# Accumulators of one PSUM bank, sums of squares added as they come, and three smaller edits in an encoder block

## The chip, the cores and the metric

The kernel runs on one core of a Trainium2 chip. Its time is the device time of one execution, in microseconds (us), and the median of several runs is what counts. Engines are called PE (TensorE, matmuls), ACT (ScalarE), DVE (VectorE), POOL (GpSimd) and SP (SyncE, which issues the DMAs).

## What is computed

One layer of an encoder on 256 positions with 2048 features, in float32. In short:

```
def reference(x, ...):
    hn = rmsnorm(h, mix_norm_pre)
    z, xbc, dt_raw, u = split(hn @ w_in)              # 1024, 1536, 32, 1024 columns
    y_ssd  = ssd_mixer(z, xbc, dt_raw, ...)            # scan in both directions, 16 heads
    y_pool = pool_mixer(u, pool_w, pool_scale)         # centred means of 4 widths, minus u
    h = h + rmsnorm(concat(y_ssd, y_pool) @ w_out, mix_norm_post)
    hn = rmsnorm(h, ffn_norm_pre)
    gate, val = split(hn @ w_ffn_up)                   # 5632 columns each
    ff = (gelu(dwconv(gate)) * val) @ w_ffn_down
    h = h + rmsnorm(ff, ffn_norm_post)
    g = sigmoid(rmsnorm(h, ple_norm_pre) @ w_ple_gate)
    return h + rmsnorm(g * (p @ w_ple), ple_norm_post)
```

`rmsnorm` divides each position by the root of the mean of its squares. All weights come from HBM in float32.

## The kernel before

Every product is made of three: a float32 matrix is split into a high part (cast on ACT, tiles `...whi`) and the rest (subtracted on DVE, `...wlo`), and PE multiplies high by high, high by low and low by high. Activations are split in the same way by `put` (ACT writes `...h`, DVE `...l`). Raw weights come by DMA from SP into four buffers (`raw`); the parts go to five buffers each.

The stages in order of time: the first product `dtu` (the columns `dt` and `u` of `w_in`), `xbc` in three slabs (2, 0, 1), `z`, the output projection `wo` (accumulator `woa`), the FFN's up projection (`ug` and `uv`, accumulators `ga` and `va`), the down projection `dn` (accumulators `dna`, `dns`), and the gate (`gt`). `ple` is a small product that does not depend on the rest and lies between these stages.

Matmuls write to PSUM, which has eight banks of 512 float32 a partition. `main` and `pair_of_banks` give tiles of two banks, of which there are three; `misc` gives one of two tiles of one bank. The program is written in order; dependences and the order on each engine are made by the framework, which tracks who reads and writes a tile as a whole: a reader of one half of a tile can be held by a writer of the other half. Beside the long products, small jobs (the list `work`, one entry a unit of the product) are called by `aside`: `pool_mix` makes the pooled means (`mx`), `pool_map` their product (`pw`), `seg(i)` one pair of exponent matrices, which share the two `misc` tiles with them.

`sublayer` makes `wo` and `dn`. It works on two halves of the 2048 columns, and in each on two blocks `t` of 128 positions and two banks `n`. For each bank ACT squares the accumulator and sums it (`woj`, sum in `woq`) and DVE multiplies it by the gain (`wom`). After both halves `rms` adds four sums for each block on POOL (L366, tiles `wo0m`, `wo1m`) and raises the result to the power −1/2 (L369, `wo0r`, `wo1r`). Then DVE adds the scaled result to `h` (L820), PE transposes `h` (`woxt`, for `dn` `dnxt`), and `put` makes the panel (`wox`, `dnx`) for the next product. `row_rstd` sums the squares of the new `h` on ACT (`rfj`), and `along_tokens` turns the factor into a row (`rfbw`, `rfbp`).

`feature_pairs` makes 256 columns of the up projection for all positions: its accumulator holds high and low products of 256 positions each beside one another in each bank, and `total` adds them: ACT copies one part out of PSUM, DVE adds the other.

## Time and profile before

| | |
|---|---|
| Time, median of 3 runs | 1131.77 us (1130.02, 1131.77, 1133.52) |
| Profiled execution | 1130.95 us, its span 1129.2 us |
| Busy: PE, DVE, ACT, POOL | 1112.7, 798.6, 662.1, 52.0 us |
| Chain that ended last: PE, DVE, ACT, DMA | 92%, 3%, 3%, 1% |

In the rows of the profile the first number of a timeline row is its start in us from the start of the span, the second its duration; then come engine, line, operation, names of output and inputs, shapes, and in brackets how long the engine had been idle before and which engine and tile it waited for. A row with "x8" stands for eight instructions. Windows give start and end, the length, then busy time and instruction count of PE, PE's weight loads, DVE, ACT and POOL, then the clock, the DMA share and GB/s. Rows of waits give total time, how often, and the longest. Rows of grouped instructions (by line and shape) give the total busy time in us, the mean of one in ns, and idle time before them. Rows of loads give the KB of each and the median us from issue to landing.

### The profile page before, as it was taken

To read this page: it belongs to the slowest core of one execution; us is meant where nothing else is said; L and a number is where in the kernel's file an instruction comes from. 1 tells how busy PE (TensorE), PEld (TensorE's weight loads), DVE (VectorE), ACT (ScalarE), POOL (GpSimd) and SP (SyncE) were. 2 spreads that over 40 slices of the span, in tenths; PEclk is the share of its full clock that TensorE was granted. 3 is DMA by queue.
4 is the path that set the end of the run, shared out by engine and by line. 5 is a ranking of instruction groups with operands and counts; after the bars stand their busy time and mean duration, and the time that the engine had idled before them with its cause. 6 is when DMAs were issued, how large, how long until landed. Compare 5 with 4: busy or idle time off the path is not lost.

```text
span 1129.2 us, 15491 instructions
## 1 busy us (share of the span) xinstructions
PE 1112.7 (99%) x6031; PEld 968.1 (86%) x6031; DVE 798.6 (71%) x937; ACT 662.1 (59%) x933; POOL 52.0 (5%) x80
## 2 busy tenths in 40 slices
PE   9999999999899999999999999999999999999996
PEld 9999988888788888888888888888888888887885
DVE  6658877754767777767767676666777778787573
ACT  6747774543675565655656555646656466567462
POOL 0300023100100000000000000000000000001001
PEclk9999999999999999999999999999999999999998
DMA  9944356666577878887797697666788788885742
GB/s 354 385 153 150 114 184 203 234 185 198 187 259 253 270 263 254 264 296 250 254 318 246 224 319 259 196 196 201 258 291 284 251 276 322 302 286 192 238 135 75
DMA packets 143993, 270.43 MB, mean 239 GB/s; under 512 B 5296, under 2 KB 98352, under 8 KB 140592
## 3 DMA queue, kind: packets, MB, share of 16 engines
q1 hardware_dynamic: 143632, 269.09, 71.0%
q8 instruction: 47, 0.77, 0.3%
q10 hardware_dynamic: 288, 0.36, 0.1%
q14 instruction: 26, 0.21, 0.1%
HBM read 247.93 MB, written 21.50 MB: 239 GB/s over the span
## 4 chain that ended last, share of the span: by engine, by line
PE 92%; DVE 3%; ACT 3%; DMA 1%; issue 1%; POOL 1%; POOLq 0%; DVEq 0%; ACTq 0%
PE va L91 22%; PE ga L91 21%; PE dna L91 15%; PE woa L91 7%; PE gt L91 7%; PE xbc L91 6%; PE dns L91 5%; PE z L91 4%; PE dtu L91 2%; DMA dtur<-w_in 1%; PE pw L91 1%; PE yd L91 1%; DVE h_back L820 0%; PE seg L91 0%; ACT rxj L395 0%
## 5 line engine op out<-in xcount | busy, mean ns | idle before, releaser
L91 PE MATMUL ga<-wox,ug_0whi 128*128 128x512 f32 x352 | 88.6, 394 | 1.5 <-DVE wox L201 1.5
L91 PE MATMUL va<-wox,uv_0whi 128*128 128x512 f32 x352 | 87.6, 391 | 0.0
L91 PE MATMUL ga<-wox,ug_1whi 128*128 128x512 f32 x352 | 87.5, 390 | 0.0
L91 PE MATMUL va<-wox,uv_1whi 128*128 128x512 f32 x352 | 87.0, 390 | 0.0
L91 PEld LDWEIGHTS va<-wox,uv_1whi 128*128 128x128 f32 x352 | 66.1, 188 | 13.7
L91 PEld LDWEIGHTS ga<-wox,ug_1whi 128*128 128x128 f32 x352 | 66.0, 188 | 13.6
L91 PEld LDWEIGHTS ga<-wox,ug_0whi 128*128 128x128 f32 x352 | 64.9, 190 | 14.0 <-DVE wox L201 1.7
L91 PEld LDWEIGHTS va<-wox,uv_0whi 128*128 128x128 f32 x352 | 64.7, 188 | 12.5
L91 PE MATMUL ga<-wox,ug_1wlo 128*128 128x256 f32 x352 | 50.2, 284 | 0.0
L91 PE MATMUL ga<-wox,ug_0wlo 128*128 128x256 f32 x352 | 49.5, 283 | 0.0
L91 PE MATMUL va<-wox,uv_1wlo 128*128 128x256 f32 x352 | 49.4, 284 | 0.0
L91 PE MATMUL va<-wox,uv_0wlo 128*128 128x256 f32 x352 | 49.3, 283 | 0.0
L91 PEld LDWEIGHTS ga<-wox,ug_0wlo 128*128 128x128 f32 x352 | 46.8, 191 | 1.7
L91 PEld LDWEIGHTS va<-wox,uv_0wlo 128*128 128x128 f32 x352 | 46.7, 191 | 1.7
L91 PEld LDWEIGHTS ga<-wox,ug_1wlo 128*128 128x128 f32 x352 | 45.6, 192 | 0.3 <-ACT wox L200 0.3
L91 PEld LDWEIGHTS va<-wox,uv_1wlo 128*128 128x128 f32 x352 | 45.4, 192 | 0.0
L91 PE MATMUL xbc<-hnh,xb_0whi 128*128 128x256 f32 x96 | 28.1, 293 | 0.2 <-DVE u L539 0.2
L91 PE MATMUL xbc<-hnh,xb_1whi 128*128 128x256 f32 x96 | 27.5, 286 | 0.0
L366 POOL TENSOR_SCALAR dn0m<-dnq,fmean 128x1 f32<-128x1 f32 x1 | 0.3, 264 | 589.9 <-ACT dnj L810 589.9
L91 PE MATMUL xbc<-hnh,xb_0wlo 128*128 128x256 f32 x96 | 27.3, 285 | 0.0
L91 PE MATMUL xbc<-hnl,xb_1whi 128*128 128x256 f32 x96 | 27.2, 283 | 0.0
L91 PE MATMUL xbc<-hnh,xb_1wlo 128*128 128x256 f32 x96 | 27.2, 283 | 0.0
(1427 smaller groups left out, 3016.0 us busy)
## 6 DMA issues: line engine op xcount, KB each, us to landing
dn0r<-w_ffn_down SPq DMA_DIRECT2D x16, 1024.0 KB, 6.8
dn1r<-w_ffn_down SPq DMA_DIRECT2D x15, 1024.0 KB, 6.4
br<-w_ffn_down SPq DMA_DIRECT2D x13, 1024.0 KB, 5.6
bm<-block SPq DMA_DIRECT2D x13, 1024.0 KB, 6.3
zr<-w_in SPq DMA_DIRECT2D x8, 1024.0 KB, 5.3
wo0r<-w_out SPq DMA_DIRECT2D x8, 1024.0 KB, 6.0
wo1r<-w_out SPq DMA_DIRECT2D x8, 1024.0 KB, 5.6
gt0r<-w_ple_gate SPq DMA_DIRECT2D x8, 1024.0 KB, 5.9
```

Of the source, the lines that this page charges most:

```text
L91: nc.tensor.matmul(o, lhsT, rhs, start=start, stop=stop, skip_group_check=True)
L366: nc.gpsimd.tensor_scalar(m, q, scale, base, op0=ALU.mult, op1=ALU.add)
```

## The change

Accumulators from `main` become two tiles of one bank each, of which the pool has six, where there were three of two banks. `pair_of_banks` goes; `feature_pairs` writes to `acc[f]`, and `total` works on each bank by itself. `sublayer` adds each sum of squares on POOL as it comes and takes the power behind the last sum of each block. One `seg` stands in each unit of `xbc`, and `pool_map` is spread with it. The second part of `x` (`xt1`) lies in one of the four raw weight buffers. `pool_mix` has its matmuls put behind the last matmul ahead of it in the program.

```
--- before.py
+++ after.py
-            tc.tile_pool(name="pmain", bufs=3, space=bass.MemoryType.PSUM) as pm, \
+            tc.tile_pool(name="pmain", bufs=6, space=bass.MemoryType.PSUM) as pm, \
...
         def main(name):
-            t = pm.tile([P, 1024], F32, tag="main", name=name)
-            return [t[:, :512], t[:, 512:]]
-
-        def pair_of_banks(name):
-            return pm.tile([P, 1024], F32, tag="main", name=name)
+            return [pm.tile([P, 512], F32, tag="main", name=f"{name}_{i}") for i in range(2)]
...
         def mm(o, lhsT, rhs, start, stop):
-            nc.tensor.matmul(o, lhsT, rhs, start=start, stop=stop, skip_group_check=True)
+            last["pe"] = ins(nc.tensor.matmul(o, lhsT, rhs, start=start, stop=stop, skip_group_check=True))
...
-        xt = [ep.tile([P, V_SCW + L], F32, name="xt0")] + [page(f"xt{i}") for i in (1, 2)]
+        xt = [ep.tile([P, V_SCW + L], F32, name="xt0")] + [wp.tile([P, 2048], F32, tag="raw", bufs=4, name="xt1"), page("xt2")]
...
         def total(o, acc):
 
-            v, w = o.rearrange("p (f t) -> p f t", f=2), acc.rearrange("p (f q t) -> p q f t", f=2, q=2)
-            nc.scalar.copy(v, w[:, 1])
-            nc.vector.tensor_add(v, v, w[:, 0])
+            for f in range(2):
+                nc.scalar.copy(o[:, f * L:(f + 1) * L], acc[f][:, L:])
+                nc.vector.tensor_add(o[:, f * L:(f + 1) * L], o[:, f * L:(f + 1) * L], acc[f][:, :L])
...
         def pool_mix(g):
             ps = misc(f"mx{g}")
+            behind = last["pe"]
             for c in range(2):
                 for s, (t0, t1) in enumerate(((0, P + 8), (P - 8, L))):
-                    mm(ps[:, c * L + t0:c * L + t1],
-                       ut[:, s * 1024 + g * 256 + c * P:s * 1024 + g * 256 + (c + 1) * P],
-                       pmat[:, (2 * g + s) * L + t0:(2 * g + s) * L + t1], s == 0, s == 1)
+                    with tc.issue_after(behind):
+                        mm(ps[:, c * L + t0:c * L + t1],
+                           ut[:, s * 1024 + g * 256 + c * P:s * 1024 + g * 256 + (c + 1) * P],
+                           pmat[:, (2 * g + s) * L + t0:(2 * g + s) * L + t1], s == 0, s == 1)
...
         work.extend([
-            [job(seg, 0), job(seg, 1), job(pool_map, 0), job(pool_map, 1)],
+            [job(seg, 0), job(pool_map, 0)],
+            [job(seg, 1), job(pool_map, 1)],
             [job(seg, 2), job(cb, bc, 0), job(cb, bc, 1)],
-            [job(seg, 3), job(seg, 4), job(pool_map, 2)],
-            [job(seg, 5), job(pool_map, 3)],
+            [job(seg, 3), job(pool_map, 2)],
         ])
         xa = xbc(0)
         work.extend([
-            [job(seg, 6), job(scale_by_dt, 0, 0, 0)],
-            [job(seg, 7), job(scale_by_dt, 0, 0, 1), job(weigh, 0, 0)],
-            [job(xs_turn, xa, 0)],
-            [],
+            [job(seg, 4), job(pool_map, 3), job(scale_by_dt, 0, 0, 0)],
+            [job(seg, 5), job(scale_by_dt, 0, 0, 1), job(weigh, 0, 0)],
+            [job(seg, 6), job(xs_turn, xa, 0)],
+            [job(seg, 7)],
         ])
...
             mg = [page(f"{name}m{t}") for t in range(2)]
-            sq = [[], []]
+            mean, r = list(base), []
             for half in range(2):
...
                         nc.scalar.activation(junk, b, AF.Square, accum_out=q)
                         nc.vector.tensor_mul(mg[t][:, c], b, gain[:, c])
-                        sq[t].append(q)
+                        m = tiny(f"{name}m{t}{half}{n}", 1)
+                        nc.gpsimd.tensor_scalar(m, q, 1.0 / D, mean[t], op0=ALU.mult, op1=ALU.add)
+                        mean[t] = m
+                    if half:
+                        r.append(tiny(f"{name}r{t}", 1))
+                        nc.gpsimd.tensor_tensor(r[t], mean[t], mhalf[:, :1], op=ALU.pow)
             if ahead:
                 ahead()
-            r = [rms(f"{name}{t}", sq[t], 1.0 / D, 1, base[t]) for t in range(2)]
             pan = panel(f"{name}x")
```

In `feature_pairs`, `acc[:, f * 512:(f + 1) * 512]` becomes `acc[f]`, and `ga` and `va` come from `main`. Lines move by up to four.

On PE, the place between `dtu` and the first slab of `xbc`: `rxbp` turns the factors of the first norm, `mx` is the pooling. Before:

```order
L91 MATMUL rxbp<-ident,rxbw_607 128x128
L91 MATMUL rxbp<-ident,rxbw_610 128x128
L91 MATMUL mx_764<-pmat,u 128x136
L91 MATMUL xbc_647<-hnh_115,xb_0whi 128x256
L91 MATMUL xbc_647<-hnl_117,xb_0whi 128x256
```

After:

```order
L87 MATMUL rxbp<-ident,rxbw_610 128x128
L87 MATMUL rxbp<-ident,rxbw_613 128x128
L87 MATMUL xbc_0_650<-hnh_118,xb_0whi 128x256
L87 MATMUL xbc_0_650<-hnl_120,xb_0whi 128x256
L87 MATMUL xbc_0_650<-hnh_118,xb_0wlo 128x256
```

The `mx` matmul no longer stands ahead of the first `xbc` matmul; all of them come behind the unit.

On PE, the end of the output projection. `woxt` are transposes of `h` (before `h_2068` is block 0 and `h_2069` block 1, after `h_2076` and `h_2077`). Before, the 22 `ple` matmuls from the end of `woa` to the first transposes, of which the last rows are shown:

```order
L91 MATMUL ple_2798<-ple_0whi,pth 128x512
L91 MATMUL ple_2798<-ple_0wlo,pth 128x512
L91 MATMUL ple_2798<-ple_0whi,ptl 128x512
L91 MATMUL ple_2798<-ple_1whi,pth 128x512
L380 MATMUL woxt_2718<-ident,h_2068 128x128
L380 MATMUL woxt_2727<-ident,h_2068 128x128
L91 MATMUL ple_2798<-ple_1wlo,pth 128x512
L91 MATMUL ple_2798<-ple_1whi,ptl 128x512
L380 MATMUL woxt_2718<-ident,h_2069 128x128
L380 MATMUL woxt_2718<-ident,h_2068 128x128
L380 MATMUL woxt_2718<-ident,h_2069 128x128
L380 MATMUL woxt_2727<-ident,h_2069 128x128
```

After, from the last `woa` matmul on:

```order
L87 MATMUL woa_1_2423<-wo_1whi,catl_2071 128x512
L376 MATMUL woxt_2730<-ident,h_2076 128x128
L376 MATMUL woxt_2739<-ident,h_2076 128x128
L87 MATMUL ple_0_2809<-ple_0whi,pth 128x512
L87 MATMUL ple_0_2809<-ple_0wlo,pth 128x512
L87 MATMUL ple_0_2809<-ple_0whi,ptl 128x512
```

And, still on PE, after these and seven more `ple` matmuls:

```order
L87 MATMUL ple_1_2810<-ple_1wlo,pth 128x512
L87 MATMUL ple_1_2810<-ple_1whi,ptl 128x512
L376 MATMUL woxt_2730<-ident,h_2077 128x128
L376 MATMUL woxt_2730<-ident,h_2076 128x128
L376 MATMUL woxt_2730<-ident,h_2077 128x128
L376 MATMUL woxt_2739<-ident,h_2077 128x128
```

Two transposes of block 0 now stand right behind `woa`, and 12 `ple` matmuls lie between them and the transposes of block 1.

On DVE, the same place. `wom` is the accumulator times the gain (before `wom_2074` is block 0 and `wom_2075` block 1, after `wom_2082` and `wom_2083`), `ug_..wlo` are splits of the FFN's first weights. Before:

```order
L811 TENSOR_TENSOR wom_2074<-woa_2402,gmix 128x512 x2
L157 TENSOR_TENSOR ug_1wlo<-ug00r_2902,ug_1whi 128x1024
L811 TENSOR_TENSOR wom_2075<-woa_2403,gmix 128x512
L157 TENSOR_TENSOR ug_0wlo<-ug00r_2944,ug_0whi 128x1024
L811 TENSOR_TENSOR wom_2075<-woa_2403,gmix 128x512
L820 SCALAR_TENSOR_TENSOR h_2068<-wom_2074,wo0r,h_2068 128x512
L820 SCALAR_TENSOR_TENSOR h_2069<-wom_2075,wo1r,h_2069 128x512
L820 SCALAR_TENSOR_TENSOR h_2068<-wom_2074,wo0r,h_2068 128x512
```

After:

```order
L809 TENSOR_TENSOR wom_2082<-woa_0_2420,gmix 128x512
L809 TENSOR_TENSOR wom_2082<-woa_1_2421,gmix 128x512
L822 SCALAR_TENSOR_TENSOR h_2076<-wom_2082,wor_2708,h_2076 128x512 x2
L809 TENSOR_TENSOR wom_2083<-woa_0_2422,gmix 128x512
L822 SCALAR_TENSOR_TENSOR h_2076<-wom_2082,wor_2708,h_2076 128x512
L809 TENSOR_TENSOR wom_2083<-woa_1_2423,gmix 128x512
L822 SCALAR_TENSOR_TENSOR h_2077<-wom_2083,wor_2722,h_2077 128x512 x3
L197 SCALAR_TENSOR_TENSOR wox_2724<-woxt_2730,vt,wox_2724 128x256
```

The first two updates of `h` of block 0 stand ahead of block 1's `wom`, and the two splits between the `wom` rows have moved behind all of `h` and the first four `wox`.

More of the change, by code (lines that the diff above doesn't have):

```diff
@@ L336, in high @@
                     for k, f, s in block(u, j):
-                        mm(acc[:, f * 512:(f + 1) * 512], wh[:, s], get.both(k), k == 0, False)
+                        mm(acc[f], wh[:, s], get.both(k), k == 0, False)
             def low(u, tiles):
@@ L341, in low @@
                     for k, f, s in block(u, j):
[L342 removed]
+                        mm(acc[f][:, L:], wl[:, s], get(k)[0], False, False)
             def block(u, j):
@@ L910, in build @@
             for i in range(2):
-                ga = pair_of_banks(f"ga{s}{i}")
+                ga = main(f"ga{s}{i}")
                 feature_pairs(f"ug{s}{i}", w_up, s * 512 + i * 256, hf, ga)
@@ L924, in build @@
             for i in range(2):
-                va = pair_of_banks(f"va{s}{i}")
+                va = main(f"va{s}{i}")
                 feature_pairs(f"uv{s}{i}", w_up, DFF + s * 512 + i * 256, hf, va)
```

1 line of the change is left out of this document (removed).

## The prediction

> **What bounds the kernel now.** I read the page first, then busy time by stage, then PE's waits, then the timeline at the places where it waits.
>
> ```profile
> PE 1112.7 (99%) x6031; PEld 968.1 (86%) x6031; DVE 798.6 (71%) x937; ACT 662.1 (59%) x933; POOL 52.0 (5%) x80
> 46.00:145.00 99.00, 97.78 (x739) 94.27 (x739) 71.34 (x119) 66.50 (x115) 0.40 (x2) 1.00 0.50 169
> 290.00:330.00 40.00, 36.15 (x196) 29.89 (x195) 30.57 (x46) 28.21 (x46) 5.33 (x11) 0.96 0.69 230
> 330.00:794.00 464.00, 464.00 (x2678) 411.30 (x2677) 328.37 (x363) 268.15 (x360) 0.00 (x0) 1.00 0.78 255
> 1017.00:1040.00 23.00, 22.12 (x110) 17.42 (x109) 19.84 (x31) 15.41 (x31) 3.65 (x8) 1.00 0.57 179
> PE ga L91 <- DVE wox L201: 1.5, 1, 1.5
> PE woxt L380 <- DVE wox L201: 1.5, 3, 0.8
> PE rfbp L91 <- DVE rfbw L406: 0.5, 1, 0.5
> PE mx L91 <- ACT u L538: 0.3, 1, 0.3
> PE xbc L91 <- DVE u L539: 0.2, 1, 0.2
> ```
>
> The first row is busy time over the span of 1129.2 us: PE works 99% of it, so work that lies beside PE is free and a gain has to come out of PE's idle time. The windows show where that is. In the FFN, 330 to 794 us, PE is busy 464.00 of 464 us. It is idle for 3.85 us between 290 and 330 (from the output projection to the FFN), 1.22 between 46 and 145, 0.88 between 1017 and 1040, and for the rest at the two ends. The waits name them: the transposes and first products behind `wox`, one row each for `rfbp`, `mx` and `xbc`. The change leaves the number of matmuls alone, so its whole effect has to appear in these few us, or as new idle time.
>
> The profiled execution took 1130.95 us against 1131.77, the median of the runs. I make the sum in its times and take the difference from the median.
>
> **The start of xbc.** `pool_mix` no longer puts the first `mx` matmul in front of `xbc`, and `xbc`'s first bank needs one reader gone, not all four of a two-bank tile.
>
> ```profile
> 52.54 0.61 PE L91 MATMUL rxbp<-ident,rxbw 128*128 128x128 f32 x4
> 52.90 0.53 ACT L538 ACTIVATE u<-dtu,rx0r 128x320 f32<-128x320 f32 x1 [1.98 <-DVE dt L537]
> 53.46 0.58 DVE L539 TENSOR_SCALAR u<-dtu,rx0r 128x352 f32<-128x352 f32 x1 [0.52 <-ACT u L538]
> 53.48 0.50 PE L91 MATMUL mx<-pmat,u 128*128 128x136 f32 x2 [0.33 <-ACT u L538]
> 54.19 0.36 PE L91 MATMUL xbc<-hnh,xb_0whi 128*128 128x256 f32 x1 [0.21 <-DVE u L539]
> ```
>
> PE ends `rxbp` near 53.0, waits for ACT's `u` (52.90) to do `mx`, then for DVE's `u` (53.46) to free the tile of `xbc`, which starts at 54.19. In the new order `xbc` stands right behind `rxbp`, and its bank is that of `dtu2` for token block 0 (the first 128 tokens), whose `u` is now ACT's first: the matmuls of that block stand 1.4 us ahead of `rxbp` in PE's order, so the bank is free. Start 53.0 in place of 54.19, less 0.23 for the two `mx` matmuls that PE does later: 0.96 us. The exponent pairs are spread one to a unit, and `pw0` takes the place of the second pair behind the same ACT copy, so I leave the other stalls of this stage (1.22 idle in all, counting the 0.54 above) as they are. Bounds: −0.2, if they grow by what the start wins, to −1.8, if all idle time but small change goes.
>
> **From the projection to the FFN.** Accumulators of one bank let the first sum of squares start when its own bank is done; the mean is built as sums come, the power follows the last sum of its block, and in DVE's new order `h` stands ahead of the splits of `ug`.
>
> ```profile
> 284.08 0.39 PE L91 MATMUL woa<-wo_1whi,catl 128*128 128x512 f32 x1
> 285.93 0.60 ACT L810 ACTIVATE woj<-woa 128x512 f32<-128x512 f32 x1 [1.73 <-PE woa L91]
> 287.38 0.60 ACT L810 ACTIVATE woj<-woa 128x512 f32<-128x512 f32 x1 [0.76 <-DVE wom L811]
> 288.23 0.26 POOL L366 TENSOR_SCALAR wo0m<-woq,wo0m 128x1 f32<-128x1 f32 x1 [1.17 <-ACT woj L810]
> 288.58 0.57 POOL L369 TENSOR_TENSOR wo0r<-wo0m,mhalf 128x1 f32<-128x1 f32 x1
> 288.16 0.39 PE L91 MATMUL woa<-wo_1whi,catl 128*128 128x512 f32 x1
> 289.05 1.23 DVE L157 TENSOR_TENSOR ug_1wlo<-ug00r,ug_1whi 128x1024 fp32r<-128x1024 f32 x1 [0.26 <-ACT ug_1whi L156]
> 289.23 1.09 POOL L366 TENSOR_SCALAR wo1m<-woq 128x1 f32<-128x1 f32 x1
> 292.52 0.74 DVE L820 SCALAR_TENSOR_TENSOR h<-wom,wo0r,h 128x512 f32<-128x512 f32 x1
> 292.58 1.10 POOL L369 TENSOR_TENSOR wo1r<-wo1m,mhalf 128x1 f32<-128x1 f32 x1
> 293.72 0.75 DVE L820 SCALAR_TENSOR_TENSOR h<-wom,wo1r,h 128x512 f32<-128x512 f32 x1 [0.45 <-POOL wo1r L369]
> 296.91 1.15 PE L91 MATMUL ga<-wox,ug_0whi 128*128 128x512 f32 x2 [1.51 <-DVE wox L201]
> 310.41 1.97 ACT L395 ACTIVATE rfj<-h 128x2048 f32<-128x2048 f32 x1
> 313.79 0.46 PE L91 MATMUL rfbp<-ident,rfbw 128*128 128x128 f32 x2 [0.52 <-DVE rfbw L406]
> ```
>
> Today bank 0's last matmul starts at 284.08, yet its `woj` waits until 285.93, when bank 1 is done; bank 1's `woj` waits for DVE's `wom` of bank 0, to 287.38. So `wo0r`, the factor of token block 0, comes at 289.15, the first columns of `h` of block 0 at 293.26 (behind two splits and `wom`), those of block 1 at 294.47.
>
> Step by step after: `woj` of bank 0 at 284.5, of bank 1 at 285.9, 1.45 before today's 287.38, and the factor with it: 287.7. `h` of block 0, now next on DVE, is written by 288.5 (0.74 each), when PE leaves `woa` (288.55): its two transposes hardly wait. Block 1: its last `woj` stands behind one cast on ACT and ends near 289.75; the mean step and the power, between the rows with and without a neighbour on DVE (0.26 to 1.09 and 0.57 to 1.10), give its factor between 290.7 and 292.1. I take 291.2, one of the two at the long row, and `h` of block 1 at 292.0. PE fills until 291.5 with 12 `ple` matmuls and waits 0.5. The 6 transposes, 11 `ple`, 8 more transposes and 8 `ga` then run to about 298.1 without a gap (today `ga` starts at 296.91 with 8 transposes fewer done). What is late next: the splits of `ug`, moved behind, now stand before the `wox` for which the transposes `woxt8` wait, 1.2 us more. ACT reaches `rfj`, the row sums of `h`, some 2.1 us sooner than 310.41, since its `wox` and `pl` come sooner. So `rfbp` starts at 311.7 and not at 313.79, and in the new order five matmuls of 512 columns and one of 256 more stand ahead of it (5 × 0.227 + 0.12 = 1.25 us by the distance of their starts): 2.1 + 1.25 = 3.3 us. Bounds: −1.5, if the next wait on DVE takes all but the transposes that need no wait, to −4.2, a bit over the idle time of this window with the refill after each wait.
>
> **From the down projection to the gate.** The same change of `sublayer`.
>
> ```profile
> 1020.31 0.60 ACT L810 ACTIVATE dnj<-dna 128x512 f32<-128x512 f32 x1 [0.93 <-DVE dnm L811]
> 1025.67 0.74 DVE L820 SCALAR_TENSOR_TENSOR h_back<-dnm,dn0r,h_back 128x512 f32<-128x512 f32 x1
> 1026.00:1030.00 4.00, 3.48 (x18) 2.30 (x17) 4.00 (x8) 3.42 (x6) 0.00 (x0) 1.00 0.99 357
> 1035.37 0.73 PE L91 MATMUL gt<-gt_1wlo,dnxh 128*128 128x512 f32 x2 [0.36 <-DVE gt_1wlo L157]
> ```
>
> `h_back` could start at about 1024.1 in place of 1025.67, but DVE is full (4.00 of 4.00 us), so an earlier `h_back` only pushes the split of `gt_0` (1.21 us) behind it, and the 17 `ple` matmuls that cover this place stay as many. PE begins its transposes 1.5 us sooner and then waits for `gt_0wlo` and the next `dnxl`, where it waits for a split today (1035.37). I count 0; −1.2 if the idle time here goes, +0.9 if the split costs a wait of its own size less what is won.
>
> **Edits costed at nothing.** `total` makes two copies and two additions of 256 columns out of one each of 512, 44 times.
>
> ```profile
> L359 ACT COPY gr<-ga 128x512 f32<-128x512 f32 x22 | 12.9, 588 | 15.9 <-PE ga L91 15.9
> L200 ACT ACTIVATE wox<-woxt,vt 128x256 fp32r<-128x256 f32 x16 | 7.1, 478 | 4.1 <-PE woxt L380 3.1 <-DVE wox L201 1.0
> L360 DVE TENSOR_TENSOR gr<-gr,ga 128x512 f32<-128x512 f32 x22 | 15.1, 688 | 1.5
> L645 DVE TENSOR_TENSOR cbm<-small,cbm 128x256 f32<-128x256 f32 x4 | 1.5, 422 | 0.5 <-ACT cbm L643 0.5
> ```
>
> ACT: 2 × 0.478 − 0.588 = 0.37 us more each, DVE: 2 × 0.422 − 0.688 = 0.16. That is 16.2 us of ACT and 6.9 us of DVE, on engines with 268 and 328 of 464 us busy; the cover is PE's unbroken 464 us, and without it they cost up to 23 us (below). The Trainium skill ("VectorE: DVE Perf Modes", section on the TRN2 errata) speaks against this edit: a fixed cost is paid by each instruction, so tiles should be of 512 elements or more. Its formula for an fp32 addition, (N+151)/0.96 ns, gives 0.157 us more for each pair, an estimate that agrees with the 0.16 of the rows; the sum by it would still be 0 while PE covers it.
>
> Half of `x` in a weight buffer: the loads of the first product have one buffer less and three are issued up to 2.8 us later.
>
> ```profile
> dtur<-w_in SPq DMA_DIRECT2D x14, 528.0 KB, 10.1
> 29.77 1.08 ACT L156 CAST dtu12whi<-dtur 128x1056 fp32r<-128x1056 f32 x1
> 41.02 0.64 PE L91 MATMUL dtu<-dtu12whi,hnh 128*128 128x352 f32 x3
> ```
>
> A load takes 10.1 us from issue to landing, and the loads land one by one, so most of that is waiting behind others and a later issue moves its landing by less; and `dtu12`, cast at 29.77, is first used at 41.02. The cover is about 8 us; the price without it is what goes beyond. SP issues the first `uv` load behind two stores of `h`, but its first use is a whole pair of `ga` products away. At the end, the `tanh` of block 1's first bank could start sooner, but the last bank's chain, which ends the span, starts with the last matmul as before: 0.
>
> **Sum.** −0.96 − 3.3 + 0 = −4.3 us: 1126.7 for the profiled execution, 1127.5 on the median. 0.3%, about what a measurement here can tell from no change, is 3.4 us.
>
> **Rivals.**
>
> R1, the wait moves: with `h` of block 0 now on DVE while POOL makes block 1's factor, both of POOL's steps take the long rows, the factor comes at 292.1, and all behind it, DVE's queue included, is 0.9 later: 2.4 won in place of 3.3. At the gate it costs 0.9 in the same way. −0.96 − 2.4 + 0.9 = −2.5: 1129.3. For it speak `wo1m` (1.09) and `wo1r` (1.10) beside DVE's work on SBUF; against it that DVE, waiting for the factor, lets POOL through. The Trainium skill ("GPSIMD Engine Reference", "Key points") says that GpSimd contends with VectorE instructions with two SBUF inputs; the rows agree (0.26 beside `wom`, which reads PSUM, 1.09 beside the split), and by that rule R1 is the case.
>
> R2, slower: the FFN's covers fail. If each `total` holds the casts and splits queued behind it, and PE waits for weights by that much, 44 × (0.37 + 0.16) = 23 us: 1150.6. It decides from (3.4 + 4.3) / 44 = 0.175 us a `total` on. Against it: PE shows no wait at all in this window, and ACT and DVE idle over a quarter of it. The rule on small tiles of the Trainium skill ("VectorE: DVE Perf Modes", section on the TRN2 errata) leads to this time, were these engines the bound.
>
> R3, all idle time goes: the gate gives 1.2 and xbc 1.8: −6.3, 1125.5. For it: an earlier `h_back` by 1.5 us; against: DVE full there.
>
> **How the numbers follow.** Forecast 0.54, R1 0.26, R3 0.11, R2 0.09. The forecast's own range is −2.8 to −5.6, of which about 0.09 falls short of 3.4 us. So faster 0.45 + 0.11 = 0.56, same 0.09 + 0.26 = 0.35, slower 0.09. The range adds the bounds of the three places: −1.8 − 4.2 − 1.2 = −7.2 and −0.2 − 1.5 + 0.9 = −0.8, that is 1124.6 to 1131.0, and 0.5 on both sides for the median's own scatter (1130.02 to 1133.52 before): 1124.1 to 1131.5. It leaves out R2 and the ends of the others.
>
> **What would show it.** Right: `xbc` starting at 53.0 with no wait for `mx`; the `woj` of 285.93 at 284.5; `h` from 287.7 on; `rfbp` 2 us sooner; 330 to 794 without PE idle, two 128x256 additions near 0.42 us in it. Wrong: a wait of PE for `wox` as long as today's, `wor1` at or over 1.1 us, PE idle in the FFN, or `dtu` weights that PE waits for before 50 us.

## The result, and the profile after

The changed kernel took 1125.95 us (median of 6 runs, 1125.63 to 1127.74) beside 1131.68 for the kernel before on the same chip: a ratio of 0.9953, with a 95% interval of 0.9940 to 0.9965: about 0.5% faster, which is clear of the scatter. Its profiled execution took 1125.82 us, its span is 1124.0 us.

Where the 5.2 us of span come from is read best as distances between the same PE instructions in the two traces (start to start, from the timeline of PE). The last column is the first experiment below, the one-bank accumulators alone.

| From … to (first or last matmul of the name) | before | after | change | banks alone |
|---|---|---|---|---|
| start … first `rxbp` | 52.54 | 52.50 | −0.04 | 52.60 |
| first `rxbp` … last `z` | 144.09 | 143.60 | −0.49 | 142.83 |
| last `z` … last `woa` | 91.53 | 91.53 | 0 | 91.53 |
| last `woa` … first `va` | 38.83 | 35.32 | −3.51 | 34.33 |
| first `va` … last `va` | 466.53 | 466.53 | 0 | 466.53 |
| last `va` … last `gtz` | 326.45 | 325.39 | −1.06 | 325.27 |
| last `gtz` … end | 9.18 | 9.12 | −0.06 | 9.12 |

The row of busy times from the page, the window of the FFN and some of PE's waits in the changed kernel:

```profile
PE 1109.0 (99%) x6031; PEld 965.9 (86%) x6031; DVE 796.1 (71%) x981; ACT 665.8 (59%) x977; POOL 48.9 (4%) x80
...
326.00:790.00 464.00, 464.00 (x2678) 411.14 (x2677) 328.01 (x404) 270.58 (x402) 0.00 (x0) 1.00 0.78 255
...
PE woxt L376 <- DVE wox L197: 1.1, 2, 0.9
PE dnxt L376 <- DVE dnxl L197: 0.9, 1, 0.9
PE dtu L87 <- ACT dtu0whi L152: 0.8, 1, 0.8
```

In the FFN PE is busy 464.00 of 464 us as before, though DVE runs 404 instructions there instead of 363 and ACT 402 instead of 360. Of PE's waits, that of `ga` for `wox` (1.51) and that of `mx` are gone; `woxt` still waits 1.1 us for `wox`, `rfbp` as long as before. New are a wait of 0.9 for `dnxl` and one of 0.8 for `dtu0whi`, the first weights. The latter is one of the signs of being wrong that the prediction named; it is taken up with the experiment on `xt1`.

PE's busy time falls from 1112.7 to 1109.0 us with the same 6031 matmuls. Part of that is the clock. In the trace of the kernel before, the granted clock is 0.50 for 3.4 us behind the wait of 1.51 us. The kernel called "the rest" below has the same `sublayer`, the same order of PE's matmuls there and a wait of the same length, and keeps a clock of 1.00. A window and the transposes in it, first before, then the rest:

```profile
297.01:300.43 3.42, 3.03 (x11) 2.34 (x12) 3.35 (x7) 1.22 (x4) 0.00 (x0) 0.50 0.09 38
298.44 1.94 PE L380 MATMUL woxt<-ident,h 128*128 128x128 f32 x8 [0.39 <-DVE wox L201]
```

```profile
299.20:302.60 3.40, 2.50 (x14) 1.97 (x15) 3.40 (x8) 1.78 (x4) 0.00 (x0) 1.00 0.01 2
300.83 1.06 PE L380 MATMUL woxt<-ident,h 128*128 128x128 f32 x8 [0.81 <-DVE wox L201]
```

Eight transposes take 1.94 us in the one and 1.06 in the other, and the stretch from the last `woa` to the first `va` 38.83 and 37.89. So of the 3.51 us in the table 0.94 are the clock in the one trace of the kernel before; beside 37.89 the change wins 2.57 us there and the accumulators alone 3.56. The lower clock is no accident of that trace: the mean granted clock of an execution is 0.996 or less in 24 of 35 executions of the kernel before whose clock is on record (median 1131.9 us; 1130.1 for the other 11), and in 2 of 50 of the kernels with accumulators of one bank. Where the clock fell in those executions is not shown, but a part of the gain in the medians goes with it. Why the rest has it in none of its ten executions, in spite of the same wait, stays open.

A wait costs PE a little more than its idle time also at full clock: the pair of `ga` matmuls behind the wait of 1.51 us takes 0.73 us in the rest, a pair without a wait 0.6. So idle time alone tells less than distances do.

The three places on the timeline of the changed kernel, the start of `xbc` first:

```profile
52.50 0.61 PE L87 MATMUL rxbp<-ident,rxbw 128*128 128x128 f32 x4
52.87 0.36 PE L87 MATMUL xbc<-hnh,xb_0whi 128*128 128x256 f32 x1
53.99 0.39 PE L87 MATMUL xbc<-hnh,xb_0whi 128*128 128x256 f32 x1 [0.17 <-ACT u L534]
```

`xbc` starts right behind `rxbp`, 0.37 us after its start instead of 1.65. Six matmuls later it stops once, for a `u` that still reads the next bank.

From the projection to the FFN:

```profile
284.05 0.60 ACT L808 ACTIVATE woj<-woa 128x512 f32<-128x512 f32 x1 [0.36 <-PE woa L87]
285.35 0.60 ACT L808 ACTIVATE woj<-woa 128x512 f32<-128x512 f32 x1 [0.61 <-PE woa L87]
286.55 0.57 POOL L815 TENSOR_TENSOR wor<-wom,mhalf 128x1 f32<-128x1 f32 x1
287.15 1.42 DVE L822 SCALAR_TENSOR_TENSOR h<-wom,wor,h 128x512 f32<-128x512 f32 x2 [0.39 <-POOL wor L815]
289.19 0.78 POOL L811 TENSOR_SCALAR wom<-woq,wom 128x1 f32<-128x1 f32 x1 [1.15 <-ACT woj L808]
290.05 0.56 POOL L815 TENSOR_TENSOR wor<-wom,mhalf 128x1 f32<-128x1 f32 x1
290.64 2.08 DVE L822 SCALAR_TENSOR_TENSOR h<-wom,wor,h 128x512 f32<-128x512 f32 x3 [0.21 <-POOL wor L815]
291.45 0.88 PE L376 MATMUL woxt<-ident,h 128*128 128x128 f32 x6 [0.28 <-DVE h L822]
295.53 1.22 DVE L153 TENSOR_TENSOR ug_1wlo<-ug00r,ug_1whi 128x1024 fp32r<-128x1024 f32 x1
299.21 0.63 PE L376 MATMUL woxt<-ident,h 128*128 128x128 f32 x4 [0.91 <-DVE wox L197]
311.02 0.46 PE L87 MATMUL rfbp<-ident,rfbw 128*128 128x128 f32 x2 [0.54 <-DVE rfbw L402]
```

The first sums (`woj`) come at 284.05 and 285.35, where they came at 285.93 and 287.38. The factor of block 0 is ready at 287.1 and `h` follows at once; that of block 1 is ready at 290.6, and PE waits 0.28 for the `h` behind it. Then it runs without a gap to 299.21, where it waits 0.91 us for `wox`, behind which DVE had the split of 295.53.

From the down projection to the gate:

```profile
1020.05 0.44 PE L376 MATMUL dnxt<-ident,h_back 128*128 128x128 f32 x2
1027.75 1.06 PE L376 MATMUL dnxt<-ident,h_back 128*128 128x128 f32 x8 [0.87 <-DVE dnxl L197]
1029.18 0.74 PE L87 MATMUL gt<-gt_0wlo,dnxh 128*128 128x512 f32 x2 [0.37 <-DVE gt_0wlo L153]
```

The first transposes and the products behind them have no wait in brackets now, where before the rows had 0.22 for `h_back` and, at 1028.24, 0.24 for `dnxh`. Instead a later row of transposes waits 0.87 for `dnxl`, and the first product of `gt_0wlo` 0.37.

### The profile page after: what moved, and what is told of

Same layout as the page of the kernel before. It is cut to its first block, busy times and chain, and to the rows that moved or that the text cites. A ratio compares the mean times of both kernels' runs of the same rounds, so it can differ in the third digit from the quotient of the medians.

```text
span 1124.0 us, 15575 instructions
## 1 busy us (share of the span) xinstructions
PE 1109.0 (99%) x6031; PEld 965.9 (86%) x6031; DVE 796.1 (71%) x981; ACT 665.8 (59%) x977; POOL 48.9 (4%) x80
## 4 chain that ended last, share of the span: by engine, by line
PE 92%; DMA 3%; ACT 2%; DVE 1%; issue 1%; POOL 0%; SPq 0%; POOLq 0%; DVEq 0%; ACTq 0%
PE va L87 22%; PE ga L87 21%; PE dna L87 16%; PE woa L87 8%; PE gt L87 7%; PE xbc L87 6%; PE dns L87 5%; PE z L87 4%; DMA dtur<-w_in 2%; DMA x<-x 1%; PE pw L87 1%; PE ple L87 1%; PE yd L87 1%; PE mx L87 0%; PE yo L87 0%
## 5 line engine op out<-in xcount | busy, mean ns | idle before, releaser
L87 PE MATMUL xbc<-hnl,xb_0whi 128*128 128x256 f32 x96 | 27.1, 282 | 0.0
```

The costliest lines, as they stand in the source:

```text
L87: last["pe"] = ins(nc.tensor.matmul(o, lhsT, rhs, start=start, stop=stop, skip_group_check=True))
```

## The experiments

### The change taken apart: accumulators, sums, the rest

The first kernel has the one-bank accumulators alone (with the `total` that they need):

```
         def main(name):
-            t = pm.tile([P, 1024], F32, tag="main", name=name)
-            return [t[:, :512], t[:, 512:]]
+            return [pm.tile([P, 512], F32, tag="main", name=f"{name}_{i}") for i in range(2)]
```

> Before, with the accumulators of one bank and the split total alone; sums of squares, pool_mix, seg and xt1 as before. If both edits of sublayer are needed for the gain (A): woj starts at its own bank's end, near 284.5, but the factors still come one after the other behind all sums and h stays behind most of the splits on DVE; first va about 1.5 us sooner than 327.00, time 1130 to 1131. If the banks alone carry the gain (C): first va 3 us or more sooner, time near 1127.5. If the 44 pairs of instructions of total cost PE time (R2): PE idle between 330 and 790, time above 1132.

The second has the sums alone, on accumulators of two banks (the edit of `sublayer`, word for word that of the change):

```
-                        sq[t].append(q)
+                        nc.gpsimd.tensor_scalar(m, q, 1.0 / D, mean[t], op0=ALU.mult, op1=ALU.add)
...
+                    if half:
+                        nc.gpsimd.tensor_tensor(r[t], mean[t], mhalf[:, :1], op=ALU.pow)
```

> Before, with the sums of squares added as they come and the power behind the last sum of each block, alone; accumulators of two banks. A: woj still waits for the whole tile (285.93, 287.38), so the factor of block 0 stays near 289, but h of block 0 is no longer behind two splits: first va about 2 us sooner than 327.00, time 1129 to 1130. If the order alone carries the gain (B): first va 3.5 us or more sooner, time near 1127.5 or below.

The third has both:

> Before, with both edits of sublayer (banks and sums) and none of the others. A and B: wo to FFN and gate as in the changed kernel, first va 3.5 us sooner than 327.00, and xbc's start gains a part by the banks; time 1126 to 1127.5. If the smaller edits carry over 1 us: above 1127.5.

The fourth has the other three edits (`pool_mix` behind, one `seg` a unit, `xt1` in a raw buffer) on accumulators of two banks:

> Before, with pool_mix behind its unit, one seg a unit and half of x in a weight buffer, and neither edit of sublayer. Prediction: mx no longer ahead of xbc, but xbc's two-bank tile still waits for its readers of dtu, so xbc starts at 53.7 rather than 54.19; last z 0.2 to 0.5 us sooner, time 1131.2 to 1131.6. If these edits carry half of the changed kernel's gain: 1129. If the weight buffer held by x delays the first product's weights: PE waits for dtu before 50 us and the time is above 1132.

| Kernel | us (median) | ratio to before, 95% | first `rxbp` … last `z` | last `woa` … first `va` | last `va` … last `gtz` |
|---|---|---|---|---|---|
| before | 1131.68 | | 144.09 | 38.83 | 326.45 |
| change | 1125.95 | 0.9953 (0.9940–0.9965) | 143.60 | 35.32 | 325.39 |
| accumulators | 1123.87 | 0.9936 (0.9921–0.9952) | 142.83 | 34.33 | 325.27 |
| sums | 1131.05 | 0.9999 (0.9990–1.0008) | 144.09 | 37.97 | 327.09 |
| accumulators and sums | 1125.03 | 0.9946 (0.9930–0.9962) | 142.84 | 35.33 | 326.01 |
| the rest | 1134.14 | 1.0023 (1.0014–1.0033) | 146.50 | 37.89 | 326.99 |

One part of the change makes all of the gain and more. The accumulators give 1.26, 4.50 and 1.18 us at the three places, of which 0.94 at the second are the clock in the trace before. The sums alone change nothing that the runs can tell: behind `wo` they take 37.97 us where the rest, with the old `sublayer` and full clock, takes 37.89, and behind `dn` 0.64 more than before and 0.10 more than the rest. Their ten executions show the price of the clock once more: five took 1130.0 to 1130.5 us at a mean clock of 0.997 or 0.998, five 1131.6 to 1131.9 at 0.996. Added to the accumulators the sums cost 1.0 us behind `wo`; of the 0.7 more at the gate in that trace 0.6 is a wait of `dna` for `dn_0wlo`, which is taken up with the gate below. The rest, by itself, makes the kernel 0.2% slower.

Of what was expected of these four, the case "banks alone carry the gain" came out, with a time 3.6 us under the 1127.5 it gave. The sums were expected 2 us sooner at the first `va` and at 1129 to 1130 us, and both edits together at 1126 to 1127.5: both were missed, the second from below. The rest was expected 0.2 to 0.5 us faster in `xbc` and lost 2.4 there.

What the sums do to DVE is seen when its timeline with the accumulators alone is laid beside that of the change:

```profile
287.80 1.23 DVE L153 TENSOR_TENSOR ug_1wlo<-ug00r,ug_1whi 128x1024 fp32r<-128x1024 f32 x1 [0.35 <-ACT ug_1whi L152]
289.54 0.74 DVE L816 SCALAR_TENSOR_TENSOR h<-wom,wo0r,h 128x512 f32<-128x512 f32 x1
290.20 0.75 DVE L816 SCALAR_TENSOR_TENSOR h<-wom,wo1r,h 128x512 f32<-128x512 f32 x1
...
293.61 0.63 PE L87 MATMUL ga<-wox,ug_0whi 128*128 128x512 f32 x2
297.62 0.63 PE L376 MATMUL woxt<-ident,h 128*128 128x128 f32 x4 [0.42 <-DVE wox L197]
299.54 0.63 PE L376 MATMUL woxt<-ident,h 128*128 128x128 f32 x4 [0.37 <-DVE wox L197]
```

Here DVE puts the split `ug_1wlo` (1.23 us) at 287.80, while ACT and POOL make the last sum and factor of block 1, and `h` of both blocks follows alternately from 289.54, though the factor of block 0 was there at 286.45. In the change `h` of block 0 stands in that place (287.15, though that run is 0.7 us behind this one at the last `woa`), and the split goes to 295.53, in front of the `wox` that PE waits for. But a tile of `wox` has both blocks in it, and the factor of block 1 comes no sooner: its power starts 0.08 us behind its last sum in both. An early `h` of one block buys nothing, and the split that made room for it is paid for later: PE's waits for `wox` are 0.42 and 0.37 us here, 0.91 and 0.18 in the change, where `h` adds 0.28.

The rest, on two-bank accumulators, shows why `xbc` needs the accumulators:

```profile
54.38 0.39 PE L91 MATMUL xbc<-hnh,xb_0whi 128*128 128x256 f32 x1 [1.25 <-DVE u L539]
158.66 0.73 PE L91 MATMUL z<-z_0wlo,hnh 128*128 128x512 f32 x2 [0.65 <-DVE z_0wlo L157]
183.75 0.44 PE L91 MATMUL yd<-xs,E 128*128 128x64 f32 x2 [0.41 <-DVE y L710]
```

`pool_mix` no longer stands ahead of `xbc`, yet `xbc` starts at 54.38 as late as before, after 1.25 us of idle time: the two `mx` matmuls had filled a part of a wait that was there anyway, for the last reader of the two-bank tile. And two waits of 0.65 and 0.41 us appear further on. Which of the three edits brings them is not shown. The sign that was named for the weight buffer is there too, a wait of PE for `dtu0whi` of 0.89 us at 6.27, but PE reaches `rxbp` at 52.52, as before, so the 2.41 us lost in this trace lie behind it.

### Which line of the sums costs the time

Sums as they come on POOL, but both powers after the loop, where they stood:

```
-                    if half:
-                        r.append(tiny(f"{name}r{t}", 1))
-                        nc.gpsimd.tensor_tensor(r[t], mean[t], mhalf[:, :1], op=ALU.pow)
...
+            for t in range(2):
+                r.append(tiny(f"{name}r{t}", 1))
+                nc.gpsimd.tensor_tensor(r[t], mean[t], mhalf[:, :1], op=ALU.pow)
```

> Banks and sums as they come, as in the third run, but the two powers stand behind both blocks and both halves again. That run and the one with banks alone differ by 1.2 us. If the place of the power is what costs (it lets DVE write three pieces of block 0's h before block 1's first, and PE's wox tiles need a piece of both blocks): h alternates between the blocks again, first va 34.3 us behind last woa as with banks alone, time 1123.5 to 1124.3. If POOL's sums in between cost: 35.3 us and 1125, as in the third run.

It took 1124.24 us, ratio 0.9936 (0.9921 to 0.9951), and 34.50 us from the last `woa` to the first `va`. With the power back DVE's order is that of the accumulators alone again:

```profile
287.50 1.23 DVE L153 TENSOR_TENSOR ug_1wlo<-ug00r,ug_1whi 128x1024 fp32r<-128x1024 f32 x1 [0.35 <-ACT ug_1whi L152]
289.42 2.74 DVE L820 SCALAR_TENSOR_TENSOR h<-wom,wor,h 128x512 f32<-128x512 f32 x4
```

The split stands ahead of `h` once more. So of the 1.0 us, 0.83 lie in the place of the power in the program, which sets the order on DVE; the sums on POOL by themselves account for at most 0.17.

### Two of the smaller edits undone

The change with the old list of jobs of `xbc` (two `seg` in two of the units):

> The changed kernel with the jobs of xbc in the old list (two pairs of exponents in the first unit, and so on); all else as changed. If the spread of seg costs the 0.7 us that the changed kernel loses between the first xbc and the last z against banks alone: last z near 195.4 instead of 196.11, time 1125.2. If it is the place of the mx matmuls: no change, 1125.9.

It took 1126.28 us, ratio 0.9952 (0.9937 to 0.9967). Its stretch from the first `rxbp` to the last `z` is 142.84 us, that of the accumulators alone, and 0.76 below the profiled execution of the change. In the other three traces with one `seg` a unit (the change again, and the two next below) it is 143.18, 143.18 and 143.19, without the wait for `u` at 53.99: so 0.35 of the 0.76 is the spreading of `seg`, and 0.4 is that wait, which one execution had and the others not. Of the 0.7 us that the text above puts to the spread, half is. The time is no lower; in the profiled execution, of 1127.03 us, PE reached `rxbp` at 53.92 and not at 52.50.

The change with `xt1` in a page of its own, as before:

```
-        xt = [ep.tile([P, V_SCW + L], F32, name="xt0")] + [wp.tile([P, 2048], F32, tag="raw", bufs=4, name="xt1"), page("xt2")]
+        xt = [ep.tile([P, V_SCW + L], F32, name="xt0")] + [page(f"xt{i}") for i in (1, 2)]
```

> The changed kernel with xt1 back in a page, so that four raw buffers are free for weights from the start. Prediction: no difference, last dtu within 0.1 us of 52.34, time within 0.5 us of 1125.95. If the buffer held by x costs: the wait of PE for dtu0whi (0.8) or later ones goes and the time is up to 1 us less.

It took 1125.61 us, ratio 0.9947 (0.9932 to 0.9962); by the times alone it is the change again. The traces show more. On ACT, first in the change, then in this kernel:

```profile
5.31 0.51 ACT L196 ACTIVATE hnh<-xt,xt 128x256 fp32r<-128x256 f32 x1 [0.55 <-DMA xt<-x_cols]
5.72 0.85 ACT L152 CAST dtu0whi<-dtur 128x352 fp32r<-128x352 f32 x2
```

```profile
4.89 0.87 ACT L152 CAST dtu0whi<-dtur 128x352 fp32r<-128x352 f32 x2 [0.29 <-DMA dtur<-w_in]
5.67 0.51 ACT L196 ACTIVATE hnh<-xt,xt 128x256 fp32r<-128x256 f32 x1
```

With `xt1` in a raw buffer, ACT's order puts an `hnh`, which has to wait for a part of `x`, ahead of the second and third cast of `dtu0whi`; with `xt1` in a page the casts come first. PE waits for these casts 0.77 to 1.76 us in all five traces with `xt1` in a raw buffer, and at most 0.39 in the nine others. So what was expected if the buffer costs did happen: the wait of 0.8 is gone here, and the last `dtu` starts at 52.09, not within 0.1 of 52.34. What the wait costs in the end differs: of the five, two reach `rxbp` at 52.50 and 52.52, inside the 52.05 to 52.60 of the nine others, and three at 53.92, 54.35 and 54.67. The edit is not free, then: beside the latest of the nine it cost nothing in two of these traces and 1.3 to 2.1 us in three.

### Double the cost that was called free

`total` cut once more, into four copies and four additions of 128 columns:

```
             for f in range(2):
-                nc.scalar.copy(o[:, f * L:(f + 1) * L], acc[f][:, L:])
-                nc.vector.tensor_add(o[:, f * L:(f + 1) * L], o[:, f * L:(f + 1) * L], acc[f][:, :L])
+                for i in range(2):
+                    s = slice(f * L + i * P, f * L + (i + 1) * P)
+                    nc.scalar.copy(o[:, s], acc[f][:, L + i * P:L + (i + 1) * P])
+                    nc.vector.tensor_add(o[:, s], o[:, s], acc[f][:, i * P:(i + 1) * P])
```

> The changed kernel with total cut once more: four copies and four additions of 128 columns, 88 more instructions each on ACT and DVE. By the rows (128 columns on DVE 0.285 us) about 0.15 us more of DVE and 0.3 to 0.5 of ACT a total. If PE covers it: no idle time of PE between 326 and 790, time 1125.5 to 1126.5. If the cover ends (R2): 44 times 0.3 us or more, 1139 or above.

It took 1127.21 us, ratio 0.9958 (0.9942 to 0.9975). Grouped instructions in the FFN, first of the change, then of this kernel, and this kernel's window:

```profile
L355 ACT COPY gr<-ga 128x256 f32<-128x256 f32 x40 | 12.9, 376 | 9.4 <-PE ga L87 9.4
L356 DVE TENSOR_TENSOR gr<-gr,ga 128x256 f32<-128x256 f32 x40 | 14.9, 414 | 0.0
```

```profile
L357 ACT COPY gr<-ga 128x128 f32<-128x128 f32 x80 | 18.4, 268 | 10.0 <-PE ga L87 10.0
L358 DVE TENSOR_TENSOR gr<-gr,ga 128x128 f32<-128x128 f32 x80 | 19.1, 280 | 0.0
326.00:790.00 464.00, 464.00 (x2677) 411.11 (x2677) 339.20 (x488) 280.47 (x485) 0.00 (x0) 1.00 0.78 255
```

DVE and ACT carry some 10 us more each than in the change, and PE is busy 464.00 of 464 us in both; from the first to the last `va` it takes 466.53 us in every trace of this study. The profiled execution took 1128.16 us, and it lost at the front: PE waited 1.76 us for its first weights and reached `rxbp` at 54.67. From there to the end of the span it took 1071.68 us, the two traces of the change 1071.50. Whether the front also makes the 1.3 us by which the median lies above the change, its trace alone cannot show. The Trainium skill ("VectorE: DVE Perf Modes", section on the TRN2 errata) gives an fp32 addition (N+151)/0.96 ns, an estimate of 0.424 and 0.291 us at 256 and 128 columns; the rows measure 0.414 and 0.280. Its advice to tile by 512 elements or more is right about the engine's time and has no bearing on the kernel's while PE covers it.

### What the accumulators still leave, and all on one chip

Two kernels go on from the accumulators alone. The first moves PE's two products `rfbp` behind the first `ga` products, through a new argument of `along_tokens`:

```
-        rfb = along_tokens("rfb", rf)
...
+                if i == 0 and s == 0:
+                    rfb = along_tokens("rfb", rf, last["pe"])
```

> Accumulators of one bank as in the first experiment, and PE's two products rfbp, which turn the factor of the norm into a row, stand behind the first ga products and not ahead of them. Theory (PE waits 0.67 us for rfbw at rfbp and nothing behind it needs the row before the first gelu): the wait goes, the stretch from the last woa to the first va gets 0.6 to 0.7 shorter than with the accumulators alone (34.3 us there), 1123.2 us. Rival: the first total then waits for the row, the two PSUM banks of the first ga come free late, and PE waits at the third pair in place of rfbp: same time as with the accumulators alone, 1123.9.

The second also takes the PSUM tiles of `seg` from the six accumulators instead of the two small tiles that it shared with `mx` and `pw`:

```
-            ps = [misc(f"seg{i}{d}") for d in range(2)]
+            ps = main(f"seg{i}")
```

> The former, and the PSUM tiles of the exponent pairs (seg) come from the six one-bank accumulators in place of the two small tiles. Theory: the two small tiles, shared by seg, mx and pw, are what PE waits for in xbc (0.79 us at 89.6 us and a few of 0.18): 0.8 to 1.1 us less from rxbp to the last z, 1122.3. Rival: an xbc or z product then waits for an accumulator that seg holds, and the gain is given back or turns into a loss of up to 1 us: 1123.2 to 1124.2.

And, to compare them on one chip, the accumulators alone and the change as it is, once more:

> The accumulators alone once more, on the same chip as the changed kernel as a whole, because the earlier comparison of the two was across chips. Theory (the other four edits cost some 2 us together): 1123.9, ratio 0.993, and 1.5 to 2.5 us under the changed kernel. Rival (the 2 us were the chip or the front of the run): within 0.7 us of it.

> The changed kernel as it is, beside the three above on one chip. Theory: 1126.0, ratio 0.995, slower than the accumulators alone by 1.5 to 2.5 us. Rival: within 0.7 us of them.

| Kernel (one chip, 5 runs each) | us (median, range) | ratio to before, 95% | `rxbp` … `z` | `woa` … `va` |
|---|---|---|---|---|
| before (9 runs) | 1131.60 (1129.85–1133.41) | | | |
| change | 1126.65 (1125.53–1127.64) | 0.9959 (0.9946–0.9971) | 143.18 | 35.32 |
| accumulators | 1123.85 (1123.07–1124.54) | 0.9933 (0.9921–0.9946) | 142.85 | 34.35 |
| … and `rfbp` moved | 1124.71 (1122.90–1124.79) | 0.9934 (0.9921–0.9947) | 142.84 | 33.53 |
| … and `seg` moved | 1121.08 (1121.00–1121.78) | 0.9908 (0.9895–0.9922) | 140.95 | 33.53 |

Every run with the accumulators alone is faster than every run of the change, by 2.8 us in the median, on one chip: the chip is not the reason. The front is a part of it. The spans of the two traces differ by 3.32 us, and 2.30 of them lie ahead of `rxbp` (52.05 and 54.35), where the change has ACT's late casts; behind it the other edits cost 1.02 us in this pair of traces and 1.89 in the pair of the first table. Moving `rfbp` shortens its stretch by 0.82 us, a little more than expected, in both traces that have it, and no wait takes its place. Its time does not show this: the five runs fall into 1122.9 (two) and 1124.7 to 1124.8 (three), and the trace is of one of the two, so whether the 0.8 us last in every run is open by the times alone. Moving `seg` wins more than was expected, 1.9 us in its stretch, and 1.8 in time beside the two runs at 1122.9:

```profile
90.52 0.50 PE L87 MATMUL seg<-seg_x,seg_w 128*128 128x512 f32 x1 [0.63 <-ACT E L601]
52.60:195.43 142.83, 142.17 (x947) 129.97 (x946) 108.81 (x164) 92.39 (x167) 15.36 (x9) 1.00 0.49 168
```

```profile
52.59:193.54 140.95, 140.95 (x947) 129.69 (x946) 108.48 (x164) 91.93 (x167) 15.37 (x9) 1.00 0.50 170
```

The first fence is of the accumulators alone: a wait for ACT's `E` (the exponent, which reads a small tile), and PE busy 142.17 of 142.83 us. In the second, of the last kernel, PE is busy all of 140.95 us with the same 947 matmuls. That wait is under half of the gain (0.79 us by the distance of the starts around it). The rest is in stops too short to be named: by distance, some 17 steps of PE in this stretch of the accumulators alone are 0.1 us or more longer than the median step of matmuls with the same operands, about 3.0 us together, and 6 in the last kernel, 0.9 us together. This version, at 0.9908, is the fastest of the study, faster than the kernel before and than the change.

## Why the prediction was right, and where its steps were wrong

It said 1127.5 us and faster as the likeliest; the time is 1125.95, inside its range, and 1.55 us below. In span: −4.3 forecast, −5.2 measured. The direction and the main mechanism, that a reader no longer waits for the whole two-bank tile, are borne out. That the sum came so close is in part luck: errors of opposite sign at `xbc` and the gate, and 0.94 us of clock in the term that looks best.

- **The start of `xbc`: forecast −0.96, measured −0.49.** The start itself came as forecast, 52.87 against 53.0, and by distance it won 1.28 (1.65 to 0.37), more than the 0.96. What failed is "so I leave the other stalls of this stage" as they are: the spread of `seg` costs 0.35, and 0.4 is a wait for `u` of the second bank. The second trace of the change is without that wait and has −0.91. The reason was also put too wide: the accumulators alone bring the early start, and `pool_mix` behind, alone, does not.
- **From the projection to the FFN: forecast −3.3, measured −3.51.** By steps: the first `woj` at 284.05 (284.5 forecast, and this run was 0.5 ahead at the last `woa`); `h` of block 0 at 287.15 (287.7); the wait for `h` of block 1 0.44 by the distance of the starts around it (0.5); the split in front of `wox` 1.1 (1.2); `rfbp` at 311.02 (311.7). The sum is right by the trace that it was made from, and two things behind it are not. First, that trace has the lower clock: 0.94 of the 3.51 is that, which the prediction does not mention, though its window from 290 to 330 has a clock of 0.96, and beside a trace at full clock the change wins 2.57. Second, the attribution. The text gave the gain to the accumulators and to `h` standing ahead of the splits; taken apart, the accumulators give 4.50 (3.56 without the clock), and the sums with the new order of `h` take 1.0 away. The prediction had both sides of it in hand, 1.2 us more because "the splits of `ug`, moved behind, now stand before the `wox`", and did not ask what the time would be without that move.
- **From the down projection to the gate: forecast 0, measured −1.06.** This term is mis-sized, and the trace of the change flatters it. The mechanism was told right (transposes sooner, then waits for `dnxl` and `gt_0wlo`, as the rows at 1027.75 and 1029.18 show), but the waits that go were taken to be worth no more than those that come. Counted from each start to the next start on PE, so that a wait falls to the matmul ahead of it, the 32 transposes took 3.80 us in place of 4.79, and the `gt` products 0.63 more. Another part lies where the prediction did not look, in the middle of the down projection. Before, PE starts the second half's first matmul 0.45 us after the start of the first half's last one, in the change 0.23. With three smaller delays behind it that is 0.47 us; all three traces with two-bank accumulators have it, and none of the eleven with one bank. The 771 `dna` matmuls took 0.59 us less, the transposes 0.99 less, `gt` 0.63 more: with 0.1 of small change that is the −1.06. But the accumulators also bring a new wait there. On DVE, first before, then in the change, and on PE in the second trace of the accumulators alone:

```profile
945.21 1.23 DVE L157 TENSOR_TENSOR dn_0wlo<-dn1r,dn_0whi 128x1024 fp32r<-128x1024 f32 x1 [1.20 <-ACT dn_0whi L156]
946.35 1.22 DVE L222 TENSOR_TENSOR dn118f<-dn1r 128x1024 f32<-128x1024 f32 x1
```

```profile
941.84 1.23 DVE L218 TENSOR_TENSOR dn118f<-dn1r 128x1024 f32<-128x1024 f32 x1 [2.73 <-DMA dn1r<-w_ffn_down]
942.98 1.22 DVE L153 TENSOR_TENSOR dn_0wlo<-dn1r,dn_0whi 128x1024 fp32r<-128x1024 f32 x1
```

```profile
942.99 0.74 PE L87 MATMUL dna<-dn_0wlo,hidh 128*128 128x512 f32 x2 [0.47 <-DVE dn_0wlo L153]
```

In the kernel before, DVE makes `dn_0wlo` first; in every kernel with one-bank accumulators `dn118f` stands ahead of it and waits for a load. Where the load lands late, PE waits for `dn_0wlo`: 0.1 to 1.0 us by distance in nine of the eleven traces, and nothing in the profiled executions of the change and of the accumulators alone, the two in the first table. The second trace of the change has −0.66 in this stretch, that of the accumulators −0.38. Rival three, which gave the gate 1.2, came nearest on this term and was wrong about `xbc`.
- **`total` at nothing: right**, and the experiment with twice as many instructions agrees. The additions took 0.414 us (0.422 forecast), the copies 0.376 (0.478), so even the bill of rival two was too high (0.16 and 0.14 us a `total` and engine, in place of 0.37 and 0.16). That rival is refuted: PE has no idle time in the FFN.
- **`xt1` at nothing: not borne out.** The step that failed is that only the issue of later loads was asked about. That part holds: in the change later loads of `dtur` are issued up to 3.1 us later than with `xt1` in a page, and land 0.3 us later, with no wait of PE. But the edit also changes ACT's order, and PE waits 0.77 us and more for `dtu0whi`, which is the sign "`dtu` weights that PE waits for before 50 us". In the profiled execution this cost nothing at `rxbp` (−0.04), in the second trace 1.81 us.
- **The tail at nothing: right** (−0.06).
- **Rival one, POOL's steps stretched:** refuted. `wom` of block 1 took 0.54 and 0.78 us and its power 0.56, not 1.1 each; the factor was there at 290.6, not 292.1. The Trainium skill ("GPSIMD Engine Reference", "Key points") has GpSimd contend with VectorE instructions of two SBUF inputs, and the rows still agree: the step of 0.54 ran beside `h`, which reads two SBUF tiles, as did that of 0.78, steps beside `wom` took 0.26. What was wrong in the rival is the size, and that the power would meet such work: it ran beside `wom`.

## What to carry to other kernels

A tile is what the framework waits for: an accumulator of two banks makes the reader of the first bank wait for the writer of the second, and the writer of either for all four readers. Split it, and the hand-overs between stages get shorter (here by 1.26, 3.56 at full clock, and 0.4 to 1.2 us), while the extra instructions cost nothing where the bounding engine has no gap. The Trainium skill ("Perfetto Trace Analysis", "Optimizing Tensor Performance") says that independent groups of matmuls should rotate through PSUM banks so that one is emptied while the next is filled; here both banks were in rotation already, only the tile tied them together, and untying them gave 0.9936: the runs agree with the rule.

Making one of two inputs early is worth nothing if the consumer needs both, and the work that it displaces has to go somewhere: look for it ahead of the next wait. An edit can also change the order on an engine far from where it is made: here that of DVE in the down projection, and that of ACT at the start. Edits that are made together should be timed apart: here one gave over 7 us, and the others took 2 to 3 of them back. And a stretch is better measured in more than one trace, with the clock beside it.

## What was not expected of the hardware

A wait of PE at the start can cost more than its own length. In these fourteen traces PE reaches `rxbp` at 52.05 to 54.67 us, and the difference arises in the first 11 us. The three above 52.60 are all of kernels with `xt1` in a raw buffer. The timeline and a window there, of the change and then of the kernel with `total` in four parts, whose front is the same program:

```profile
6.24 1.30 PE L87 MATMUL dtu<-dtu0whi,hnh 128*128 128x352 f32 x5 [0.77 <-ACT dtu0whi L152]
7.38 1.12 PE L87 MATMUL dtu<-dtu0wlo,hnh 128*128 128x352 f32 x6
4.60:11.20 6.60, 5.83 (x33) 5.10 (x32) 4.83 (x10) 5.00 (x10) 0.00 (x0) 1.00 1.01 364
```

```profile
6.87 1.57 PE L87 MATMUL dtu<-dtu0whi,hnh 128*128 128x352 f32 x5 [1.76 <-ACT dtu0whi L152]
8.24 1.96 PE L87 MATMUL dtu<-dtu0wlo,hnh 128*128 128x352 f32 x6
4.60:11.20 6.60, 4.84 (x19) 4.32 (x18) 4.75 (x10) 4.71 (x10) 0.00 (x0) 0.74 1.02 387
```

The cast of the first weights is waited for 0.77 us in the one and 1.76 in the other, and the matmuls behind it start 0.63 us later. Then six matmuls take 1.96 us in place of 1.12, at a granted clock of 0.74 in this window in place of 1.00 (0.50 from 7.80 to 11.10), and by the time this is over the second kernel is 2.18 us behind, the 2.2 us between the two at `rxbp`. The length of the wait does not decide alone: in the change with the old list of jobs it was 0.84, and five matmuls behind it took 1.93 us in place of 1.30, with `rxbp` at 53.92. The column does not show it each time either: in that trace and in the second of the change, where five matmuls also took 1.93 us, it has 1.00 for the same window. Since such differences are of the size of the effects studied, small edits were compared by distances between PE instructions, which repeat to some 0.05 us from trace to trace where neither a wait that comes and goes nor a lower clock falls into them.
